# The weights of the first modulation: eight buffers instead of four, and their loads issued in another order

## The chip, the cores and the metric

The kernel runs on one core of a Trainium2 chip. The metric is the time of one execution in microseconds (us). Its engines are PE (TensorE: matmuls; PEld is its weight load), DVE (VectorE), ACT (ScalarE), POOL (GpSimd) and SP (SyncE, which here issues nearly all transfers between HBM and the on-chip memory, in one queue). Each engine takes its instructions in the order in which the program lists them, and waits where one of them is not ready.

## The reference, cut to what matters

One step of a two-layer trunk over T = 1152 tokens (1024 latent tokens, 128 of a prompt) with 1024 features. Of each layer only the beginning matters here:

```
mod = silu(cond) @ w_mod + b_mod                  # six sections of 1024 columns
sh1, sc1, g1, sh2, sc2, g2 = split(mod, 6)
hn  = rms_norm(x, norm1_g) * (1 + sc1) + sh1       # the normalized input
z, xbc, dt, nat_qkv, rwkv_in, diff_qkv = split(hn @ w_in)
... four mixers, an output projection, a squared-ReLU MLP, each gated by a section of mod
```

Nothing can be projected before hn is there; hn needs x, the row norms of x, and the first two sections of mod (sh1 and sc1, 2048 columns) for two conditions, that of the latent tokens and that of the prompt.

## The kernel before, in words

Features lie on the 128 partitions, tokens along the free axis: x is eight tiles of 128 features by 1152 tokens, loaded in three chunks of 384 tokens, two transfers of 768 KB a chunk. Products are made from two halves of each number (`wh`, `wl` of a weight; `h0h`, `h0l` to `h2h`, `h2l` of the normalized chunks 0 to 2), three matmuls for each product (`mm3`, lines 99 to 101).

`modulation_first` (line 169) makes the first two sections of the first layer's modulation on PE. The weights are eight pieces of 128 x 2048 (1 MB each), piece k for features 128k to 128k+127; each takes four matmuls of 512 columns (line 182), which add into four rows in PSUM over all eight pieces. Only after the last piece are the rows copied out (`mrow`), turned into columns by sixteen small transposes (line 192), and added to the bias (`md`, line 194). The pieces lie in a pool with four buffers, so pieces 4 to 7 wait until PE has read pieces 0 to 3. Then come `c_pack` (identity, ones and masks, 549 KB), and, in the program's text after the function, the six loads of x (line 1439).

`norm` does each chunk in two parts. The sums: eight squares on ACT (line 220), added up in turn on DVE and POOL (line 223), six small matmuls (line 227), the inverse root on DVE (lines 229 and 42 to 47, twelve instructions), three transposes on PE (line 233). The application: for each of eight tiles DVE multiplies (`t`, line 240), ACT adds the shift and rounds (lines 242 to 247), and DVE or POOL makes the low half (lines 245 and 248). `proj_fm` then multiplies by weight tiles; the weights come through one `raw` buffer, are split by ACT (`wh`, line 82) and POOL (`wl`, line 84), and the results leave through ACT (`st`, line 262). The first call takes three weight tiles together (72 matmuls a chunk), the second one (24 a chunk); then `proj_tm` takes a weight of two pieces (`in_w_in_tm`). After the norm, `cond_rows` loads the conditions once more (`row`, line 145), and `modulation` makes the other four sections of the first layer on DVE from 32 loads (`mod`, line 159; line 162), while PE projects. A table of relative biases is written to HBM by some twenty small transfers (lines 1152 to 1159).

The order of instructions on each engine is not that of the text: a scheduler places every instruction of the program by its own model of times and by priorities (`high_priority`). What one place changes can so move instructions elsewhere.

Of the memory: the pool `wp` (the weights being split) lies at the right end, and beside it, from `layer_input`, the pool `hn` with the six tiles of the normalized input (six of 12,288 bytes a partition), `stg`, and `nt` with the temporaries of the norm. x and the pool `m0` of `modulation_first` lie on the left.

Of the kernel before, what the change touches and what calls it, by code (L numbers as in the profile page):

```python
# [8 lines left out]
F32 = mybir.dt.float32  # L9
# [5 lines left out]
PSUM = bass.MemoryType.PSUM  # L15
# [5 lines left out]
CH3 = [(0, 384), (384, 384), (768, 384)]  # L21
# [13 lines left out]
def bcast_in(ap, n):  # L35
    return ap.unsqueeze(len(ap.shape)).to_broadcast(list(ap.shape) + [n])
# [75 lines left out]
def ps2(env):  # L112
    return env.ps_d.tile([128, 512], F32, tag="d", name="psd")
# [10 lines left out]
def psx(env):  # L124
    return env.ps_x.tile([128, 512], F32, tag="x", name="psx")
# [40 lines left out]
        nc.vector.tensor_tensor(out=md[:, s], in0=acc[:, :, :, 0], in1=bcast_in(env.bmod[:, L, s * 8:s * 8 + 8], 2), op=ALU.add)  # L166


def modulation_first(env, src, cond, md, pool, psr, pack):

    nc = env.nc
    c = pool.tile([128, 3, 8, 2], F32, name="ccol")
    nc.sync.dma_start(out=c[:, 0], in_=cond)
    nc.scalar.activation(out=c[:, 1], in_=c[:, 0], func=AF.Tanh, scale=0.5)
    nc.vector.scalar_tensor_tensor(out=c[:, 1], in0=c[:, 1], scalar=1.0, in1=c[:, 0], op0=ALU.add, op1=ALU.mult)
    nc.vector.tensor_scalar_mul(out=c[:, 2], in0=c[:, 1], scalar1=0.5)
    rows = [ps2(env), ps2(env)] + [psr.tile([128, 512], F32, name=f"psr{i}") for i in range(2)]
    for k in range(8):
        w = pool.tile([128, 2048], F32, tag="w", name="w", bufs=4)
        nc.sync.dma_start(out=w, in_=src[k])  # L180
        for o in range(4):
            nc.tensor.matmul(rows[o][0:2], c[:, 2, k], w[:, o * 512:o * 512 + 512], start=k == 0, stop=k == 7)
    nc.sync.dma_start(out=pack, in_=env.A["c_pack"])
    r = pool.tile([2, 2048], F32, name="mrow")
    ps = psx(env)
    for o in range(4):
        if o % 2:
            nc.vector.tensor_copy(r[:, o * 512:o * 512 + 512], rows[o][0:2])
        else:
            nc.scalar.activation(out=r[:, o * 512:o * 512 + 512], in_=rows[o][0:2], func=AF.Copy)  # L190
        for j in range(o * 4, o * 4 + 4):
            nc.tensor.transpose(ps[:, 2 * j:2 * j + 2], r[:, j * 128:j * 128 + 128], env.const.ident[0:2, 0:2])
    for s in range(2):
        nc.vector.tensor_tensor(out=md[:, s], in0=ps[:, s * 16:s * 16 + 16].rearrange("p (j c) -> p j c", c=2), in1=bcast_in(env.bmod[:, 0, s * 8:s * 8 + 8], 2), op=ALU.add)
# [12 lines left out]
def hidden(pool, chunks):  # L207

    return [[pool.tile([128, 8, 384], F32R, name=f"h{c}{i}") for i in "hl"] for c in chunks]
# [1176 lines left out]
def kernel(ctx: ExitStack, tc: tile.TileContext, A: dict, O: dict):  # L1386
    nc = tc.nc
    env = Env()
# [18 lines left out]
    cp = const.tile([128, 1098], F32, name="pack")  # L1407
# [10 lines left out]
    def layer_input():  # L1418

        hx, early, tx = ExitStack(), ExitStack(), ExitStack()  # L1420
        hp = hx.enter_context(tc.tile_pool(name="hn", reuse_waits="tile", bufs=1, side="right"))
        env.stg = early.enter_context(tc.tile_pool(name="stg", reuse_waits="tile", bufs=3, side="right"))
        tp = tx.enter_context(tc.tile_pool(name="nt", reuse_waits="tile", bufs=2, side="right"))
        return hidden(hp, range(3)), tp, hx, early, tx

    dense = ExitStack()
    env.wp = dense.enter_context(tc.tile_pool(name="wp", reuse_waits="tile", bufs=1, side="right"))
    H, tp, hx, early, tx = layer_input()
    left = ExitStack()
    xp = left.enter_context(tc.tile_pool(name="xp", reuse_waits="tile", bufs=1))  # L1430
    x = xp.tile([128, 8, T], F32, name="x")
    mds = [const.tile([128, 6, 8, 2], F32, name=f"md{L}") for L in range(DEPTH)]
    start = ExitStack()
    ep = start.enter_context(tc.tile_pool(name="m0", reuse_waits="tile", bufs=1))
    with tc.tile_pool(name="ps_0", reuse_waits="tile", bufs=1, space=PSUM) as ps_0:
        modulation_first(env, A["w_mod0"], A["cond_c"], mds[0], ep, ps_0, cp)
    for c0, n in CH3:
        for k in range(0, 8, 4):
            nc.sync.dma_start(out=x[:, k:k + 4, c0:c0 + n], in_=A["x"][:, k:k + 4, c0:c0 + n])

    for L in range(DEPTH):
        md = mds[L]
# [87 lines left out]
        early = ex.enter_context(tc.tile_pool(name="df_qk", reuse_waits="tile", bufs=1, side="right"))  # L1530
# [4 lines left out]
        with tc.tile_pool(name="ps_t1", reuse_waits="tile", bufs=2, space=PSUM) as ps_t, tc.tile_pool(name="ps_s3", reuse_waits="tile", bufs=1, space=PSUM) as ps_s:  # L1535
            dense, left, hx, tx, mx = ExitStack(), ExitStack(), ExitStack(), ExitStack(), ExitStack()
# [15 lines left out]
        with tc.tile_pool(name="mix", reuse_waits="tile", bufs=1) as mp:  # L1552
# [3 lines left out]
            H = hidden(hx.enter_context(tc.tile_pool(name="hn2", reuse_waits="tile", bufs=1, side="right")), range(1))  # L1556
            tp = tx.enter_context(tc.tile_pool(name="nt2", reuse_waits="tile", bufs=2, side="right"))
# [9 lines left out]
        tp = tx.enter_context(tc.tile_pool(name="nt", reuse_waits="tile", bufs=2, side="right"))  # L1567
# [23 lines left out]
        if nxt:  # L1591
            H, tp, hx, early, tx = nxt
# [142 lines left out]
```

## Time and profile before

| | |
|---|---|
| median of 3 runs | 4220.53 us (4210.94 to 4223.38) |
| the profiled execution | 4216.06 us, of which its span 4214.3 us |
| PE busy | 4039.3 us, 96% of the span |
| DVE busy | 2496.9 us, 59% |
| ACT busy | 1525.2 us, 36% |
| POOL busy | 1110.3 us, 26% |

The profile shows one execution. A busy share is an average over stages with different limits, so what a change of the first hundred microseconds is worth is read from the rows of that stage: from the timeline (each instruction's start and duration, and in brackets the idle time of its engine before it and what ended it), and from windows (busy time of each engine in a stretch, TensorE's granted clock as a share of 2.4 GHz, and what the DMA engines moved).

### The profile page before, as it was taken

The page shows a single profiled execution, that of the slowest core. Times are in us where ns is not written, and L with a number is a line of the kernel's source. Part 1 is how long each engine was busy: PE and PEld are TensorE (multiplying, and loading weights), DVE is VectorE, ACT ScalarE, POOL GpSimd, SP SyncE. Part 2 cuts the span into 40 slices and gives each one's busy share as a digit, 9 for nine tenths or more (in the row PEclk, how much of TensorE's full clock was granted, in tenths as well). Part 3 has the DMA queues.
Part 4 walks back from the last instruction along what each step waited for, and adds up shares of the span by engine and source line. Part 5 has one row for each costly group of instructions (what it writes and reads, how often), then busy time and mean ns, then how long its engine had stood idle before and what let it go on. Part 6 is the DMA issues. An engine that isn't in the chain of part 4 may idle for free.

```text
span 4214.3 us, 69091 instructions
## 1 busy us (share of the span) xinstructions
PE 4039.3 (96%) x27394; PEld 3736.9 (89%) x27394; DVE 2496.9 (59%) x5734; ACT 1525.2 (36%) x2896; POOL 1110.3 (26%) x866
## 2 busy tenths in 40 slices
PE   8899889999999999999999999899899999999999
PEld 5889777877889999999998998778777999999999
DVE  4996747678766993333346647566777463333333
ACT  4333325556644221211243233355566241111111
POOL 2243340223143211211233433302323332112111
PEclk9999989999999999999999999989899999999999
DMA  5663343322231551111144342443122301111112
GB/s 195 197 198 115 119 124 86 91 65 53 70 114 37 170 169 42 41 46 40 46 123 135 114 138 89 136 103 81 38 60 76 106 26 41 46 41 41 45 41 71
DMA packets 211187, 375.74 MB, mean 89 GB/s; under 512 B 78176, under 2 KB 144240, under 8 KB 209840
## 3 DMA queue, kind: packets, MB, share of 16 engines
q1 hardware_dynamic: 210800, 371.31, 29.1%
q8 instruction: 216, 3.54, 0.3%
q14 instruction: 107, 0.88, 0.1%
q0 software_dynamic: 64, 0.02, 0.0%
HBM read 285.33 MB, written 86.42 MB: 88 GB/s over the span
## 4 chain that ended last, share of the span: by engine, by line
PE 76%; DVE 12%; DMA 6%; issue 2%; ACT 2%; SPq 1%; POOL 1%; DVEq 0%; ACTq 0%; POOLq 0%
PE psd L99 12%; PE psd L101 12%; PE psd L100 12%; PE tps L1141 6%; PE psx L101 5%; PE psx L99 5%; PE psx L100 5%; PE tps L1129 2%; DVE junk L162 2%; PE psd L938 2%; PE S L1349 2%; DVE tm L867 1%; DMA K<-scr 1%; PE psd L930 1%; PE psd L958 1%
## 5 line engine op out<-in xcount | busy, mean ns | idle before, releaser
L84 POOL TENSOR_TENSOR wl<-raw,wh 128x1024 fp32r<-128x1024 f32 (+3 forms) x200 | 473.3, 2368 | 1533.6 <-ACT wh L82 1533.6
L82 ACT ACTIVATE wh<-raw 128x1024 fp32r<-128x1024 f32 (+3 forms) x200 | 205.7, 1031 | 770.5 <-PE psd L101 669.5
L294 DVE SCALAR_TENSOR_TENSOR x<-psd,md,x 128x384 f32<-128x384 f32 (+2 forms) x442 | 212.6, 504 | 341.2 <-PE psd L101 340.6
L101 PE MATMUL psd<-fl,wh 128*128 128x384 f32 x992 | 335.2, 338 | 0.0
L99 PE MATMUL psd<-fh,wl 128*128 128x384 f32 x992 | 334.7, 337 | 0.0
L100 PE MATMUL psd<-fh,wh 128*128 128x384 f32 x992 | 334.7, 337 | 0.0
L1141 PE MATMUL tps<-pT,V 128*128 128x128 f32 (+1 forms) x2144 | 299.2, 289 | 1.7 <-ACT pT L1136 1.6
L99 PE MATMUL psd<-h2h,wl 128*128 128x384 f32 x816 | 284.4, 349 | 11.9 <-ACT st L262 7.7
L1141 PEld LDWEIGHTS tps<-pT,V 128*128 128x128 f32 (+1 forms) x2144 | 270.5, 198 | 20.5 <-issue 3.3
L100 PE MATMUL psd<-h2h,wh 128*128 128x384 f32 x816 | 283.3, 348 | 0.0
L101 PE MATMUL psd<-h2l,wh 128*128 128x384 f32 x816 | 281.5, 346 | 0.0
L379 DVE TENSOR_TENSOR fl<-s,fh 128x384 fp32r<-128x384 f32 x192 | 209.2, 1090 | 97.8 <-ACT fh L378 97.4
L1136 ACT ACTIVATE pT<-tps 128x512 f32<-128x512 f32 (+3 forms) x368 | 166.7, 476 | 177.6 <-PE tps L1129 163.3
L99 PE MATMUL psd<-h0h,wl 128*128 128x384 f32 x592 | 206.8, 349 | 1.6 <-ACT st L262 1.3
L377 DVE SCALAR_TENSOR_TENSOR s<-psd,r 128x384 f32<-128x384 f32 x128 | 71.1, 556 | 229.1 <-ACT r L376 228.8
L99 PE MATMUL psd<-h1h,wl 128*128 128x384 f32 x592 | 204.8, 346 | 1.7 <-ACT h1h L244 1.4
L100 PE MATMUL psd<-h0h,wh 128*128 128x384 f32 x592 | 204.2, 345 | 0.0
L100 PE MATMUL psd<-h1h,wh 128*128 128x384 f32 x592 | 203.7, 344 | 0.0
L101 PE MATMUL psd<-h0l,wh 128*128 128x384 f32 x592 | 203.2, 345 | 0.0
L1355 ACT ACTIVATE e<-e,st 128x1280 f32<-128x1280 f32 x144 | 180.5, 1254 | 62.5 <-DVE st L1354 48.7
L101 PE MATMUL psd<-h1l,wh 128*128 128x384 f32 x592 | 202.3, 343 | 0.1
L294 DVE SCALAR_TENSOR_TENSOR x<-psx,md,x 128x384 f32<-128x384 f32 (+2 forms) x198 | 103.4, 538 | 161.6 <-PE psx L101 160.1
(613 smaller groups left out, 10989.3 us busy)
## 6 DMA issues: line engine op xcount, KB each, us to landing
raw<-in_w_ff_dram SPq DMA_DIRECT2D x128, 512.0 KB
mod<-in_w_mod_dram SPq DMA_DIRECT2D x80, 512.0 KB
raw<-in_w_in_fm_dram SPq DMA_DIRECT2D x42, 512.0 KB
scr<-st SPq DMA_DIRECT2D x78, 192.0 KB
scr<-x SPq DMA_DIRECT2D x26, 576.0 KB
K<-scr SPq DMA_DIRECT2D x32, 352.0 KB
K<-scr SPq DMA_DIRECT2D x64, 176.0 KB
u<-scr SPq DMA_DIRECT2D x18, 576.0 KB
```

What stands on the lines that cost most here:

```text
L82: nc.scalar.activation(out=h[:, :n], in_=raw, func=AF.Copy)
L84: nc.gpsimd.tensor_tensor(out=l[:, :n], in0=raw, in1=h[:, :n].bitcast(F32), op=ALU.subtract)
L99: nc.tensor.matmul(ps, al, bh, start=i == 0, stop=False)
L100: nc.tensor.matmul(ps, ah, bh, start=False, stop=False)
L101: nc.tensor.matmul(ps, ah, bl, start=False, stop=i == n - 1)
L162: nc.vector.scalar_tensor_tensor(out=junk, in0=w[:, i * 512:i * 512 + 512], scalar=0.5, in1=parts[c * 2 + i], op0=ALU.mult, op1=ALU.mult, ...
L294: env.nc.vector.scalar_tensor_tensor(out=x[:, kt, s0:s1], in0=ps[:, s0 - c0:s1 - c0], scalar=g[:, kt, cd:cd + 1], in1=x[:, kt, s0:s1], op0 ...
L379: nc.vector.tensor_tensor(out=fl[j][:, c0:c0 + n], in0=s, in1=fh[j][:, c0:c0 + n].bitcast(F32), op=ALU.subtract)
L938: nc.tensor.matmul(pp[:, i * 128:i * 128 + 128], B[hs, c0 + i].rearrange("p a t -> p (a t)"), A[hs, c0 + i].rearrange("p a t -> p (a t)"), ...
L1136: nc.scalar.activation(out=pT[0:g[i][1], i * 128:j * 128], in_=pp[0:g[i][1], i * 128:j * 128], func=AF.Copy)
L1141: nc.tensor.matmul(out, V[0:n, vb], parts[k // 4][0:n, k % 4 * 128:k % 4 * 128 + 128], start=k == 0, stop=k == len(kt) - 1)
L1355: nc.scalar.activation(out=e[:, :N], in_=e[:, :N], func=AF.Exp, scale=-1.0, bias=m, accum_out=st[:, 6:7] if c else s0)
```

## The change

The pieces of the modulation's weights get a pool of their own, `w0`, with eight buffers (65,536 bytes a partition). It lies on the right, and it is closed before `layer_input` is called, so that the tiles of the normalized input come to lie on the same place. The loads are listed as: pieces 0 to 3, `c_pack`, the first chunk of x, pieces 4 to 7, the second and the third chunk of x. No computation is added or taken away.

```diff
-def modulation_first(env, src, cond, md, pool, psr, pack):
+def modulation_first(env, src, cond, md, pool, wpool, psr, pack, load):
...
     for k in range(8):
-        w = pool.tile([128, 2048], F32, tag="w", name="w", bufs=4)
+        if k == 4:
+            nc.sync.dma_start(out=pack, in_=env.A["c_pack"])
+            load(0)
+        w = wpool.tile([128, 2048], F32, tag="w", name="w", bufs=8)
         nc.sync.dma_start(out=w, in_=src[k])
         for o in range(4):
             nc.tensor.matmul(rows[o][0:2], c[:, 2, k], w[:, o * 512:o * 512 + 512], start=k == 0, stop=k == 7)
-    nc.sync.dma_start(out=pack, in_=env.A["c_pack"])
+    load(1)
+    load(2)
...
-    H, tp, hx, early, tx = layer_input()
     left = ExitStack()
...
-    with tc.tile_pool(name="ps_0", reuse_waits="tile", bufs=1, space=PSUM) as ps_0:
-        modulation_first(env, A["w_mod0"], A["cond_c"], mds[0], ep, ps_0, cp)
-    for c0, n in CH3:
+
+    def load(c):
+        c0, n = CH3[c]
         for k in range(0, 8, 4):
             nc.sync.dma_start(out=x[:, k:k + 4, c0:c0 + n], in_=A["x"][:, k:k + 4, c0:c0 + n])
+
+
+    with tc.tile_pool(name="ps_0", reuse_waits="tile", bufs=1, space=PSUM) as ps_0, tc.tile_pool(name="w0", reuse_waits="tile", bufs=1, side="right") as wq:
+        modulation_first(env, A["w_mod0"], A["cond_c"], mds[0], ep, wq, ps_0, cp, load)
+    H, tp, hx, early, tx = layer_input()
```

The first place is SP's queue at the program's start, from the first pieces on (`w` are the pieces, `raw` the weight tiles of the projections). Before:

```order
L180 DMA w<-in_w_mod_dram 128x2048 x4
L183 DMA pack<-in_c_pack_dram 128x1098
L1439 DMA x<-in_x_dram 128x4x384 x4
L91 DMA raw<-in_w_in_fm_dram 128x1024
L1439 DMA x<-in_x_dram 128x4x384 x2
L180 DMA w<-in_w_mod_dram 128x2048 x4
```

and after the change:

```order
L183 DMA w<-in_w_mod_dram 128x2048 x4
L180 DMA pack<-in_c_pack_dram 128x1098
L1442 DMA x<-in_x_dram 128x4x384 x2
L183 DMA w<-in_w_mod_dram 128x2048 x2
L91 DMA raw<-in_w_in_fm_dram 128x1024
L183 DMA w<-in_w_mod_dram 128x2048 x2
L1442 DMA x<-in_x_dram 128x4x384 x4
```

The four last pieces have moved ahead of four of the six loads of x.

The second place is DVE's queue from the modulation's columns (`md`) on: `t` and `h0l` are the application of the norm to chunk 0, `sums` and `st` belong to the sums of a later chunk. Before:

```order
L194 TENSOR_TENSOR md_94<-psx,bmod 128x16 x2
L464 MEMSET sp_1333 128x72
L204 SCALAR_TENSOR_TENSOR md_94<-md_94,ng 128x16
L240 SCALAR_TENSOR_TENSOR t<-x,md_94,psm 128x384 x3
L245 SCALAR_TENSOR_TENSOR h0l<-t,md_94,h0h 128x384
```

and after the change:

```order
L198 TENSOR_TENSOR md_79<-psx,bmod 128x16 x2
L208 SCALAR_TENSOR_TENSOR md_79<-md_79,ng 128x16
L244 SCALAR_TENSOR_TENSOR t<-x,md_79,psm 128x384 x3
L227 TENSOR_TENSOR sums<-sums,sq 128x384
L249 SCALAR_TENSOR_TENSOR h0l<-t,md_79,h0h 128x384 x2
L244 SCALAR_TENSOR_TENSOR t<-x,md_79,psm 128x384 x3
L249 SCALAR_TENSOR_TENSOR h0l<-t,md_79,h0h 128x384
L227 TENSOR_TENSOR sums<-sums,sq 128x384
```

Before, all sums stood ahead of `md` on DVE; now those of chunks 1 (from its second addition on) and 2 stand between the applications.

The third place is SP's queue after the norm: `mod` are the loads of the other sections, `scr` and `in_rel_bias` the small transfers of the bias table, `scr<-st` stores of projected tiles, `in_w_in_tm` the two pieces of the weight of `proj_tm`. Before:

```order
L159 DMA mod<-in_w_mod_dram 128x1024
L1156 DMA scr_236<-in_rel_bias_dram 49x60x16
L159 DMA mod<-in_w_mod_dram 128x1024
L1159 DMA scr_236<-in_rel_bias_dram 60x16 x2
L263 DMA scr_191<-st 128x384
L1159 DMA scr_236<-in_rel_bias_dram 60x16 x4
L159 DMA mod<-in_w_mod_dram 128x1024
L263 DMA scr_192<-st 128x384
L91 DMA raw<-in_w_in_tm_dram 128x1056
```

and after the change:

```order
L159 DMA mod<-in_w_mod_dram 128x1024
L91 DMA raw<-in_w_in_tm_dram 128x1056
L1160 DMA scr_240<-in_rel_bias_dram 49x60x16
L267 DMA scr_197<-st 128x384
L159 DMA mod<-in_w_mod_dram 128x1024
L1163 DMA scr_240<-in_rel_bias_dram 60x16 x6
L159 DMA mod<-in_w_mod_dram 128x1024
L267 DMA scr_198<-st 128x384
L1163 DMA scr_240<-in_rel_bias_dram 60x16 x2
L91 DMA raw<-in_w_in_tm_dram 128x1056
```

The first piece of the weight of `proj_tm` has moved ahead of the bias table's transfers, and the second stands where the table is half written; before, the first stood there.

The scheduler also moved instructions by some tens of places on PE later on: within the first layer up to about a third of PE's instructions, and again in the second layer from a half to four fifths of them. The last fifth of PE's order is the same.

## Rows read from the trace of the kernel before

**Rows 1.** The page: span, and the chain that ended last by engine.
```profile
span 4214.3 us, 69091 instructions
...
PE 76%; DVE 12%; DMA 6%; issue 2%; ACT 2%; SPq 1%; POOL 1%; DVEq 0%; ACTq 0%; POOLq 0%
```
**Rows 2.** Timeline of SP's issues, 5 to 30 us (start, us spent issuing, line, transfer).
```profile
5.67 11.05 SPq L1439 DMA_DIRECT2D x<-in_x_dram  x4
...
18.61 2.42 SPq L1439 DMA_DIRECT2D x<-in_x_dram  x2
21.13 4.94 SPq L180 DMA_DIRECT2D w<-in_w_mod_dram  x4
```
**Rows 3.** Timeline of PE, 9 to 60 us (start, us busy, line, operation, idle before).
```profile
22.11 1.88 PE L182 MATMUL psd<-w,ccol 128*2 128x512 f32 x4
23.83 1.88 PE L182 MATMUL psr<-w,ccol 128*2 128x512 f32 x4
...
36.33 3.57 PE L182 MATMUL psd<-w,ccol 128*2 128x512 f32 x4
...
46.29 1.28 PE L227 MATMUL psm<-pack,sums 128*128 128x1 f32 x10
...
52.65 1.88 PE L182 MATMUL psr<-w,ccol 128*2 128x512 f32 x4
...
58.63 0.65 PE L99 MATMUL psd<-h0h,wl 128*128 128x384 f32 x1
```
**Rows 4.** Windows of 5 us: busy by engine, granted clock, DMA share, GB/s.
```profile
10.00:15.00 5.00, 5.00 (x8) 0.82 (x7) 0.00 (x0) 0.00 (x0) 0.00 (x0) 1.00 1.00 422
...
30.00:35.00 5.00, 1.85 (x9) 1.76 (x9) 2.84 (x11) 2.05 (x5) 2.79 (x2) 0.50 1.04 423
```
**Rows 5.** Timeline of ACT, DVE and POOL around the norm, 20 to 83 us.
```profile
20.25 0.94 ACT L220 ACTIVATE sums<-x 128x384 f32<-128x384 f32 x2 [14.29 <-DMA x<-in_x_dram]
...
24.40 0.56 DVE L223 TENSOR_TENSOR sums<-sums,sq 128x384 f32<-128x384 f32 x1 [2.22 <-ACT sq L220]
...
31.88 0.16 DVE L229 TENSOR_SCALAR st<-psm 128x3 f32<-128x3 f32 x1 [4.08 <-PE psm L227]
...
35.28 0.16 DVE L47 SCALAR_TENSOR_TENSOR st<-st 128x3 f32<-128x3 f32 x1
...
56.61 1.67 DVE L240 SCALAR_TENSOR_TENSOR t<-x,md,psm 128x384 f32<-128x384 f32 x3
...
82.36 1.16 POOL L248 TENSOR_TENSOR h2l<-t,h2h 128x384 fp32r<-128x384 f32 x1 [1.68 <-ACT h2h L247]
82.42 0.22 DVE L245 SCALAR_TENSOR_TENSOR h2l<-t,md,h2h 128x128 fp32r<-128x128 f32 x1
```
**Rows 6.** Timeline of SP's issues, 80 to 122 us.
```profile
83.78 1.66 SPq L145 DMA_DIRECT2D row<-in_cond_dram  x2
...
106.19 0.38 SPq L91 DMA_DIRECT2D raw<-in_w_in_tm_dram  x1
106.62 1.67 SPq L1159 DMA_DIRECT2D scr<-in_rel_bias_dram  x2
...
116.52 0.36 SPq L91 DMA_DIRECT2D raw<-in_w_in_tm_dram  x1
...
118.99 0.65 SPq L432 DMA_DIRECT2D um<-scr  x1
```
**Rows 7.** Timeline of ACT and PE, 108 to 124 us.
```profile
111.14 1.08 ACT L82 ACTIVATE wh<-raw 128x1056 fp32r<-128x1056 f32 x1 [10.20 <-DMA raw<-in_w_in_tm_dram]
...
121.96 0.39 PE L99 MATMUL psd<-wh,h0l 128*128 128x264 f32 x1 [3.28 <-ACT st L262]
```
**Rows 8.** Windows of 50 us: PE, PEld, DVE, ACT, POOL busy, clock, DMA.
```profile
250.00:300.00 50.00, 48.41 (x311) 45.33 (x311) 49.73 (x122) 17.62 (x26) 25.57 (x19) 1.00 0.59 194
...
350.00:400.00 50.00, 46.76 (x350) 42.88 (x349) 29.48 (x90) 12.39 (x28) 18.28 (x22) 0.97 0.22 71
```
**Rows 9.** What PE waited for, 400 to 1300 us: us in total, times, longest.
```profile
PE psm L1066 <- DVE qf L1059: 11.4, 3, 6.3
```

## Prediction, made before the changed kernel was run

> **What bounds the kernel now.** I read the page first. PE is on the chain that ended last for 76% of the span [rows 1], so the change is worth what it takes out of PE's idle time, or what it lets the engines that feed PE do sooner. The change lies in the first 60 us, so the second view is the timeline of that stretch, queue by queue.
>
> SP issues all six loads of x by 21.0 us, and only then, from 21.13 us, the last four pieces of the modulation's weights [rows 2]. PE has finished the first four pieces at 25.7 us (23.83 + 1.88) and takes up the fifth at 36.33, with its clock at 0.50, that is at 1.2 GHz, after the idle stretch from 30 to 35 us; the last piece is done at 54.5 (52.65 + 1.88) and the first projection starts at 58.63 [rows 3, 4]. Meanwhile the DMA engines are full: a share of 1.00 and 422 GB/s at 10 to 15 us, 1.04 and 423 at 30 to 35 [rows 4]. The sums of the norm start when the first half of chunk 0 lands, at 20.25 us, and the application starts at 56.61, when the modulation's columns are there; DVE ends it at 82.6 and POOL at 83.5 [rows 5]. So in the first 58 us the modulation is what is late, since its weights stand behind x. From 56 to 82 us the norm's application on DVE is late, and PE follows it.
>
> The third view is what comes behind the norm. SP can issue the loads of `row` only at 83.78, and the two pieces of the weight of `proj_tm` at 106.19 and 116.52 [rows 6]. ACT stands 10.20 us for the first of these, with the evacuation of PSUM behind it in its queue, and PE takes up work at 121.96 after another wait for that evacuation [rows 7]. Then DVE is the bound for a while: it is busy 49.73 of 50 us at 250 to 300. At 350 to 400 it has slack (29.48) and PE has little (46.76) [rows 8].
>
> **The change part by part.** It adds and removes no instruction; all it costs or gains is order.
>
> The pieces. I start from x's first half, whose place in the queue is the same and which lands at 20.25 us [rows 5]. Behind it now come the second half (0.79 MB), pieces 4 and 5 (1.05 MB each), a weight tile (0.52), and pieces 6 and 7. At 0.42 MB per us [rows 4] piece 4 lands at 20.25 + 1.84/0.42 = 24.6, piece 5 at 27.1, piece 6 at 30.9 and piece 7 at 33.4. PE needs 3.44 us for a piece at full clock (two rows that start 1.72 apart), and ends the fourth at 25.7 [rows 3]; so it needs pieces 4 to 7 at 25.7, 29.1, 34 and 37.4, and waits for none. It does not fall idle, and I take the full clock for it. The end is 25.7 + 4 x 3.44 + 1.4 for the matmuls of the sums that stand between (1.28 for five of the six in the row at 46.29) = 40.9 us, where it was 54.5: 13.6 earlier. What follows is unchanged, so `md` feeds DVE at 43.0 and the first projection starts at 45.0.
>
> The price is chunk 1 and 2 of x, which land at about 37 and 41 us, behind the pieces. The sums of both, which before were done or nearly done when `md` came, now stand among the applications of chunks 0 and 1 on ACT, DVE and POOL. On DVE the application took 82.64 - 56.61 = 26.0 us; added are six additions of 0.56 and one inverse root (from 31.88 to 35.44 at most) [rows 5]: 3.4 + 3.6 = 7.0. Without any new wait the norm would end at 43.0 + 26.0 + 7.0 = 76.0. But each square waits for the addition of the one before, and each of the twelve additions (six on DVE, six on POOL) can stand behind an application's instruction, the longest of which is the one of 1.16 on POOL [rows 5]: 12 x 1.16 = 13.9, hence 89.9. No row shows this mixture. I take a third of it, 4.6, since the chain of chunk 1 begins some six us before `md` and because ACT, which starts each step, has gaps: 80.6, that is 2.0 earlier than before. So of 13.6 us at the first projection 2.0 are left at the norm's end.
>
> The Trainium skill, "DMA: Bandwidth & Descriptors", section on queues, rings and completion order, says that each DMA engine consumes the descriptors of one queue in ring order. The landing of x at 20.25 us, 14.3 us after ACT was free, agrees, as 6.1 MB stood before and in it [rows 5]. It speaks against the change as much as for it, since chunk 1 then pays for every piece put ahead of it (4.7 MB with the weight tile, 11 us at 0.42 MB per us). If the transfers in flight shared the engines evenly instead, chunk 1 would come sooner and piece 7 only near 42 us; by my estimate the first projection would then start near 50, and the sum below would hardly change, as it goes by the norm's end and by SP's queue.
>
> Behind the norm. `row` needs the norm's memory, so it moves with its end: 83.78 - 2.0 = 81.8. Then the scheduler's new order does something of its own: the second piece for `proj_tm` now stands almost where the first one stood (106.19), with two more small transfers ahead of it (1.67) [rows 6]. So it is issued at 106.19 - 2.0 + 1.67 = 105.9 instead of 116.52, 10.6 earlier, and PE restarts at 121.96 - 10.6 = 111.4. For DVE's next work (`um`, loaded at 118.99) SP must first store a tile whose evacuation stands behind that same piece on ACT, at about 112; with two small transfers (1.67) and the 2.5 us that lay between 116.52 and 118.99 that is 116.2, 2.8 earlier.
>
> From there DVE carries its 2.8 us through its full stretch, to about 310 us; PE has a lead of 10.6 which it can use for projections that wait for nothing. Behind that stretch PE is the bound with less left to do. At 390 us the gain is thus between 2.8 and 10.6; I take the middle, 7. The buffers themselves cost nothing: `h0h` is written only after `md`, which needs all pieces read.
>
> The rest of the program does the same work. Where the scheduler has moved instructions I take zero; the nearest row for a bound is PE's wait for `qf`, 11.4 us in three waits [rows 9], which can vanish or double: 11 either way.
>
> The sum: 4216.06 - 7 = 4209 for an execution like the profiled one. That one lies 4.5 below the median of the runs shown, 4220.53, and for the median I forecast 4220.53 - 7 = 4213.5, rounded to 4213. 0.3%, about what a measurement of this kernel can tell from no change, is 12.7 us: 4207.9 to 4233.2.
>
> **The rivals.** (a) More is kept. If the additions fall into gaps, the norm ends at 76.0, 6.6 earlier; then the second piece is issued at 101.3, PE restarts 15.2 earlier, and if DVE's stretch keeps that too the median is 4205. For it: PE is nearly as full as DVE, 48.41 of 50 us at 250 to 300, so a lead should last [rows 8]. Against it: twelve additions on three queues without a wait. (b) The gain is hidden. DVE's full stretch sets the end of the first 310 us, PE's lead turns into waits for DVE behind it, and 2.8 us are left: 4218. For it speaks 49.73 of 50 us on DVE, against it the slack at 350 to 400 [rows 8]. (c) Slower. The additions of chunks 1 and 2 each wait behind two foreign instructions, one of 1.16 on POOL and one on DVE of 0.56 (a third of the 1.67 at 56.61): 12 x 1.72 = 20.6, and the norm ends at 96.6, 14.0 later than before [rows 5]. `row`, the other sections of the modulation and with them DVE's full stretch are later by as much: 4234.5, rounded to 4235. It decides from a norm's end behind 82.6; for it speaks that squares and additions go round three engines, against it that the longest of these instructions would have to stand in the way each time. (d) The pieces are not there in time, because SP's issue of them waits: it spent 11.05 us on four loads of x [rows 2]. PE then has its gap as before, 3 or 4 us shorter, and the result is that of (b).
>
> **How the numbers follow.** The forecast has 0.42, its own range 4205 to 4222 (8 us for the order elsewhere); (a) 0.25, (b) and (d) together 0.20, (c) 0.13. Faster by over 0.3% is most of (a), 0.21, and the lower end of the forecast, 0.12: 0.33. Slower by over 0.3% is most of (c), 0.09, and 0.03 from the order elsewhere: 0.12. The rest, 0.55, is no change. The range of 8 in 10 takes in the order's 11 us below (a)'s middle in part and above (b): 4196 to 4229.
>
> **What would show it.** In the profile after: pieces 4 to 7 issued before chunks 1 and 2; PE without a gap from 9 to 41 us, at full clock; the first projection near 45; chunk 0 applied from 43 on with additions between; the norm's end near 81 (76 for (a), 97 for (c)); the second piece for `proj_tm` issued near 106 and PE's restart near 111; DVE full until about 307. If the norm's end comes at 81 and the time still falls by 13 us or rises, the order of the later parts has done it, and the step "zero elsewhere" is wrong.

## The result, and the profile after

| | before | after |
|---|---|---|
| median of 6 runs each | 4221.52 us (4210.94 to 4225.26) | 4252.84 us (4249.65 to 4264.92) |
| ratio, 95% interval | | 1.0082 [1.0065, 1.0098] |
| the profiled execution | 4216.06 us | 4252.64 us |

The changed kernel is slower, by 4221.5 x 0.0082 = 34.6 us [27.4, 41.4]; I had forecast 4213 and a range of 4196 to 4229. In the lines named here, the line numbers of the new kernel are 3 to 4 higher than before (the norm's application, line 240, is line 244).

The page of the profile after answers to [rows 1]: busy time, then the chain that ended last.

```profile
span 4250.9 us, 69070 instructions
...
PE 4059.8 (96%) x27394; PEld 3750.5 (88%) x27394; DVE 2493.8 (59%) x5734; ACT 1521.2 (36%) x2896; POOL 1117.6 (26%) x866
...
PE 80%; DVE 9%; DMA 5%; issue 2%; ACT 1%; POOL 1%; SPq 1%; DVEq 0%; ACTq 0%; POOLq 0%
```

PE does the same 27,394 matmuls, but is busy 4059.8 us with them instead of 4039.3. So of the 36.6 us between the two spans 20.5 are busy time of PE, and the time is not lost in waits alone: a matmul lasts longer where TensorE's granted clock is at the lower level (1.2 GHz; the four matmuls that started at 36.33 before, in a stretch at 0.50, took 3.57 us [rows 3, 4], and such a four takes 1.88 at 1.00).

The start does what the change says. SP's issues (answer to [rows 2]) have pieces 4 to 7 from 6.87 us on, and chunks 1 and 2 of x behind them:

```profile
5.68 1.15 SPq L1442 DMA_DIRECT2D x<-in_x_dram  x2
6.87 8.50 SPq L183 DMA_DIRECT2D w<-in_w_mod_dram  x2
...
15.90 1.18 SPq L183 DMA_DIRECT2D w<-in_w_mod_dram  x2
18.14 14.07 SPq L1442 DMA_DIRECT2D x<-in_x_dram  x4
```

PE, in the timeline from 9 to 60 us (answer to [rows 3]), goes from piece 4 at 25.19 to the end of piece 7 at 38.91 + 1.88 = 40.8 without a gap, and starts the first projection at 44.19, where it was 58.63:

```profile
25.19 1.88 PE L185 MATMUL psd<-w,ccol 128*2 128x512 f32 x4
...
38.91 1.88 PE L185 MATMUL psr<-w,ccol 128*2 128x512 f32 x4
...
44.19 0.66 PE L99 MATMUL psd<-h0h,wl 128*128 128x384 f32 x1 [1.86 <-ACT h0h L248]
```

But the norm ends later. In the timeline of ACT, DVE and POOL (answer to [rows 5]) the squares of chunk 1 start at 35.79, those of chunk 2 only at 57.51, after ACT has waited until PE had read the sums of chunk 1 (`sums` has one buffer); the application of chunk 1 starts at 64.59, and the last instruction of chunk 2 ends at 88.09 + 1.16 = 89.3, where it was 83.5:

```profile
35.79 0.94 ACT L224 ACTIVATE sums<-x 128x384 f32<-128x384 f32 x2 [6.15 <-DMA x<-in_x_dram]
...
57.51 0.94 ACT L224 ACTIVATE sums<-x 128x384 f32<-128x384 f32 x2 [2.91 <-PE psm L231]
...
42.87 1.66 DVE L244 SCALAR_TENSOR_TENSOR t<-x,md,psm 128x384 f32<-128x384 f32 x3
...
64.59 1.66 DVE L244 SCALAR_TENSOR_TENSOR t<-x,md,psm 128x384 f32<-128x384 f32 x3 [2.69 <-PE psm L237]
...
88.09 1.16 POOL L252 TENSOR_TENSOR h2l<-t,h2h 128x384 fp32r<-128x384 f32 x1 [1.18 <-ACT h2h L251]
```

SP's queue follows the norm's end (answer to [rows 6]): `row` at 89.51 instead of 83.78, `um` at 124.55 instead of 118.99. The second piece for `proj_tm` is issued 2.1 us earlier than before:

```profile
89.51 1.65 SPq L145 DMA_DIRECT2D row<-in_cond_dram  x2
...
98.24 0.41 SPq L91 DMA_DIRECT2D raw<-in_w_in_tm_dram  x1
...
114.42 0.49 SPq L91 DMA_DIRECT2D raw<-in_w_in_tm_dram  x1
...
124.55 0.43 SPq L436 DMA_DIRECT2D um<-scr  x1
```

PE, which had done its projections early, waits 9.68 us behind that piece and restarts at 120.36 (answer to [rows 7]: 121.96):

```profile
119.22 1.08 ACT L82 ACTIVATE wh<-raw 128x1056 fp32r<-128x1056 f32 x1 [13.97 <-DMA raw<-in_w_in_tm_dram]
...
120.36 0.59 PE L99 MATMUL psd<-wh,h0l 128*128 128x264 f32 x1 [9.68 <-ACT wh L82]
```

The windows (answer to [rows 4, 8]) show PE's clock held up in the start, 1.00 instead of 0.50, and DVE's full stretch ending later: at 350 to 400 us it is still busy 37.22 us, where it was 29.48.

```profile
30.00:35.00 5.00, 5.00 (x20) 1.79 (x18) 0.96 (x6) 0.00 (x0) 2.07 (x1) 1.00 1.02 380
250.00:300.00 50.00, 48.15 (x306) 44.33 (x306) 48.47 (x126) 13.77 (x25) 21.17 (x18) 1.00 0.48 147
350.00:400.00 50.00, 49.47 (x357) 45.87 (x356) 37.22 (x100) 14.26 (x25) 22.05 (x24) 0.93 0.37 128
```

To see where the rest is lost I compared when each engine starts the same instruction in both traces. This is the shift of PE's matmuls (median, us, later is positive), by their time in the kernel before; e1 to e3 are experiments below:

```
time before      60-80   380-420  860-900  1350-1400  2400-2450  2800-2850  3450-3500   end
after            -11.0    +12.8    +10.9     +27.2      +27.1      +13.2      +36.6    +36.6
e1                -8.1    +11.3    +10.9     +22.5      +22.3      +25.5      +22.0    +22.0
e2                -0.7     +1.6     -3.3     +18.6      +16.7       +5.5      +23.0    +23.0
e3               -11.0     +6.6     +8.4     +13.1      +13.1      +11.5      +10.0    +10.0
```

PE is 11 us ahead at 60 us and 12.8 behind at 400. Then come three steps far from the change, in stretches whose text is the same: +16 between 870 and 1370, -14 between 2430 and 2820, +23 between 2820 and 3470. Clock and waits differ between two executions of one kernel, so such a step of one trace is a lead and not a measurement; the experiments put times on them.

### The profile page after: what moved, and what is told of

Read it like the earlier page. It is cut to its first block, busy times and chain, and to the rows that moved or that the text cites. A ratio compares the mean times of both kernels' runs of the same rounds, so it can differ in the third digit from the quotient of the medians.

```text
span 4250.9 us, 69070 instructions
## 1 busy us (share of the span) xinstructions
PE 4059.8 (96%) x27394; PEld 3750.5 (88%) x27394; DVE 2493.8 (59%) x5734; ACT 1521.2 (36%) x2896; POOL 1117.6 (26%) x866
## 4 chain that ended last, share of the span: by engine, by line
PE 80%; DVE 9%; DMA 5%; issue 2%; ACT 1%; POOL 1%; SPq 1%; DVEq 0%; ACTq 0%; POOLq 0%
PE psd L99 13%; PE psd L101 12%; PE psd L100 12%; PE tps L1145 6%; PE psx L101 5%; PE psx L99 5%; PE psx L100 5%; PE tps L1133 3%; PE S L1353 2%; PE psd L942 1%; DVE junk L162 1%; PE psd L962 1%; DVE tm L871 1%; PE psd L934 1%; DMA mod<-in_w_mod_dram 1%
```

## The experiments

The theory after the comparison: the time is lost twice, by the norm's later end in the first 130 us, and by the order that the scheduler chose for the rest of the program when the start had moved. The rival was that the lag grows by itself.

**Freezing the order.** To part the two, I wrote down the order of the instructions on every engine as the scheduler had made it for one kernel, and forced it on a part of another. In the text both kernels have the same instructions in the same sequence behind the start, so a table of places is enough:

```diff
     with _tile.TileContext(nc, schedule_with_timeline_sim=True) as tc:
         tile_hybrid_trunk_kernel(tc, A, O)
+        pin(tc)
...
+def pin(tc):          # ORDER: engine -> places, in the order of writing
...
+        for a, b in zip(order, order[1:]):
+            dep(ins[b], ins[a])      # order of issue only, no wait
```

Kernels e1 to e3 and e5 to e12 differ in the table, and in the start where that is said. The traces show that the forcing does what it says: in e6 and e12 PE, DVE and ACT start the same instructions in the same sequence as before, one by one, outside the stretch that was exchanged, and in e2 they do so up to 373 us. That the forcing costs nothing by itself was not timed alone; in e8, the kernel before up to 2840 us, PE is 2.2 us behind at 2400 to 2450 us, inside the scatter of single traces. Ratios are to the kernel before, run on the same chip in the same series (medians 4216.6 to 4219.9); behind each stands what it makes of 4219 us.

**e1, the changed kernel with the old order from 400 us on.**

> The changed kernel, but from about 400 us on every engine issues its instructions in the order that it had in the kernel before (a table of places; the order is forced by edges that wait for nothing). The first 400 us are those of the changed kernel, 12.8 us behind at 400 us. Theory A (the time is lost twice: 13 us by the start itself, and about 24 us by the order that the scheduler chose for the rest): the lag stays near 13 us to the end, 4221 + 13 = 4234 us. Rival B (the start's lag grows by itself, since all that follows works against the same buffers and queues): 4250 us or more, as the changed kernel.

**e2, the mirror of it.**

> The mirror of it: the kernel before, with its own first 400 us, and from there on the order of the changed kernel on every engine. Theory A: nothing up to 400 us, then +15 between 900 and 1300, -12 between 2450 and 2800, +23 between 2850 and 3400 us, so 4221 + 24 = 4245 us. Rival B: no change, 4221 us, within 5 us.

**e3, the changed start alone.**

> The changed kernel's start alone: its first 130 us, and from there on the order of the kernel before. Theory A1 (the lag at 400 us comes from the norm's end, 5 to 6 us later, which the row loads and DVE's full stretch carry on): 4221 + 6 = 4227 us, with a lag near 6 at 400 us. Rival A2 (it comes from the scheduler's order between 130 and 400 us): about 0 at 400 us, 4221. Rival A3 (it comes from PE's wait of 9.7 us for the second weight piece of the token projection): 10 to 13 at 400 us, 4233.

| | median of runs | ratio | us |
|---|---|---|---|
| e1 | 4227.91 | 1.0021 [1.0007, 1.0036] | +9 [3, 15] |
| e2 | 4239.14 | 1.0045 [1.0028, 1.0063] | +19 [12, 27] |
| e3 | 4227.26 | 1.0011 [0.9997, 1.0024] | +5 [-1, 10] |

The theory holds: the later order alone, behind an untouched start, costs 19 us, and without it the changed kernel loses 9. Both together give 28, at the lower end of what was measured for the change (27 to 41). In the table of shifts e1 ends 22 us behind, which looks like the rival's growing lag; but its profiled execution took 4238.33, 10 us above its median, and its growth falls into 870 to 1370 us, where every trace with the old order falls behind that of before (below). e3 says what the start is worth: 5 us by the times, which is not clear of zero, and 6.6 by the shift at 400 us, which is about the lag of the norm's end (5.6) and of `um` (6.1). PE waits there about as long for the second piece of `proj_tm` (9.24 us), and the 10 to 13 us of the third expectation don't come. That e3 has 6.6 and the changed kernel 12.8 at 400 us would be the order between 130 and 400 us (by the times 4 us, which the intervals don't resolve). Six traces whose first 400 us have the order of before scatter from -3.0 to +3.0 there, so a difference of 6 us between two traces is suggested and not shown.

**e4, a small change of another kind.** In the kernel before:

```diff
-        w = pool.tile([128, 2048], F32, tag="w", name="w", bufs=4)
+        w = pool.tile([128, 2048], F32, tag="w", name="w", bufs=3)
```

> The kernel before with three buffers for the first modulation's pieces where it had four. The start changes by little (the fourth piece is issued behind x too, and PE's wait moves, the last piece being the same), but the scheduler chooses another order for a quarter of PE's instructions up to 3200 us. Theory A (the scheduler's choice alone moves the time): a shift of 5 to 25 us of either sign that arises far from the start, in steps of some 10 us at places like 900 to 1300 or 2450 to 3400 us. Rival C (the order's choice is worth less than 5 us in all, and the 24 us are special to the changed kernel's): within 5 us of 4221.

Measured: 4232.45, ratio 1.0027 [1.0017, 1.0037], +11 [7, 16]. At 400 us it is 4.6 behind, at 860 to 900 level again, and in 1350 to 1400 it is 15.5 behind. So a small change of another kind also costs some 10 us, and rival C falls. How much of it is the order alone was not parted here: the step between 870 and 1370 us is one trace's, and old orders show 4 to 12 us there (below).

**e6, e7, e8: one stretch at a time.** The kernel before, with the changed kernel's order in one stretch only.

> The kernel before, with the changed kernel's order on every engine between 2450 and 2840 us alone (second layer). Theory A (a stretch's order has a price of its own that doesn't depend on what stands ahead): the 11 to 14 us that this stretch gave back in the changed kernel are won here, 4220 - 12 = 4208 us. Rival D (that stretch only gave back what earlier stretches had lost, as waits that were there anyway): no change, 4220 us.

> The kernel before, with the changed kernel's order on every engine between 850 and 1350 us alone (first layer). Theory A: 15 to 22 us lost in this stretch and kept, 4220 + 18 = 4238 us. Rival D: the loss is made up for behind, or comes only with what stands ahead: 4220 to 4225 us.

> The kernel before, with the changed kernel's order on every engine between 2840 and 3420 us alone (second layer). Theory A: 15 to 23 us lost in this stretch and kept, 4220 + 18 = 4238 us. Rival D: the stretch lost only what the one ahead of it had won: 4220 to 4226 us.

| | median of runs | ratio | us |
|---|---|---|---|
| e6, 2450 to 2840 us | 4205.80 | 0.9965 [0.9952, 0.9978] | -15 [-20, -9] |
| e7, 850 to 1350 us | 4230.80 | 1.0027 [1.0017, 1.0038] | +11 [7, 16] |
| e8, 2840 to 3420 us | 4244.90 | 1.0057 [1.0044, 1.0070] | +24 [19, 30] |

Rival D falls in all three: each stretch has its own price. Theory A's sizes fit in e6 and e8; e7's 11 is less than the 18 that it had. Within the intervals the prices add up (-15 + 11 + 24 = 20, e2 has 19). e6 is faster than both kernels.

The traces say the same. This is how far PE's shift against the trace of before changes over each stretch (us, from table windows like those above), by whether a kernel has the new or the old order in it:

| stretch | new order | old order |
|---|---|---|
| 870 to 1370 us | +16 to +22 (after, e2, e7) | +4 to +12 (e1, e3, e5, e6, e8 to e12) |
| 2430 to 2820 us | -14 to -7 (after, e2, e6, e10, e11) | -3 to +6 (e1, e3, e5, e7, e8, e9, e12) |
| 2820 to 3470 us | +18 to +24 (after, e2, e8) | -5 to -1 (e1, e3, e5, e6, e7, e9, e10, e11) |

New and old orders don't overlap in any of the three. In the first stretch the old orders fall behind too, so the trace of before took less time there than the others do, and part of the step of +16 was that.

What a price consists of can be seen in e8. These are PE's waits from 2840 to 3440 us before (us in total, times, longest):

```profile
PE psx L979 <- ACT st L984: 4.5, 3, 2.7
PE S L1349 <- DMA K<-scr: 3.8, 1, 3.8
PE S L1349 <- issue: 2.7, 1, 2.7
```

and these in e8:

```profile
PE tps L1129 <- POOL e L1367: 7.0, 4, 3.1
PE S L1349 <- DMA Q<-scr: 5.2, 1, 5.2
PE S L1349 <- DVE e L1352: 4.1, 5, 1.4
PE S L1232 <- DMA K<-scr: 3.7, 1, 3.7
PE psd L768 <- DMA sg<-scr: 3.5, 1, 3.5
```

A pair of loads of Q and K now stands some rows later in SP's queue, and PE waits 5.2 us for Q (1.4 before); POOL's share of the attention weights (line 1367) is asked for before it is done, four times, for 7.0 us in total (once, for 1.0, before). Each is small; what they and the longer matmuls come to together is read from the windows, columns as in [rows 8]: before

```profile
2450.00:2840.00 390.00, 365.08 (x2813) 316.46 (x2811) 234.70 (x551) 161.29 (x349) 104.35 (x108) 0.92 0.41 116
2840.00:3420.00 580.00, 546.42 (x4395) 474.36 (x4390) 406.41 (x1042) 313.23 (x591) 173.56 (x147) 0.96 0.25 68
```

the second stretch in e8, moved by its shift:

```profile
2846.00:3448.00 602.00, 556.81 (x4397) 480.65 (x4397) 407.75 (x1044) 314.09 (x592) 176.63 (x148) 0.95 0.24 65
```

Of 602 - 580 = 22 us, 556.81 - 546.42 = 10.4 are matmuls that last longer, and 11.6 idle time of PE. In e6's trace the stretch of 390 us takes 383:

```profile
2458.00:2841.00 383.00, 360.05 (x2793) 313.02 (x2793) 231.38 (x546) 158.43 (x345) 103.61 (x108) 0.93 0.42 117
```

Here 5.0 of the 7 us are busy time of PE and 2.0 idle time (its profiled execution took 4212.16, the median being 4205.80). The mean granted clock of the span goes the same way in e6, 0.969 in the mean of its runs against 0.966 in those of the kernel before; for a PE that is busy nearly always that would be worth some 0.003 x 4214 = 12.6 us (an estimate from these three numbers, each clock being rounded to 0.001). But this estimate is no account of the prices in general: in e2 the means are 0.9657 and 0.9661, which is 2 us of its 19, and e4, 11 us slower, has the higher clock (0.9666 against 0.9661).

How far one trace can be trusted is shown by e6's first stretch too, 850 to 1350 us, where its order is that of before. Before:

```profile
850.00:1350.00 500.00, 472.18 (x3829) 411.11 (x3828) 355.12 (x899) 272.10 (x502) 150.73 (x124) 0.97 0.25 71
```

e6:

```profile
849.00:1360.00 511.00, 483.15 (x3831) 420.22 (x3829) 354.40 (x898) 272.35 (x502) 150.97 (x124) 0.95 0.25 70
```

The same instructions in the same order took 11 us more, at a granted clock of 0.95 instead of 0.97. A single pair of traces had shown me +16 for the new order in this stretch; the times say +11 [7, 16].

**e12, the last stretch cut in two.**

> Where in 2840 to 3420 us the 24 us are lost: the kernel before with the changed kernel's order between 3100 and 3420 us alone. In the profile of the whole stretch 4.7 us were lost up to 3100 and 16.3 behind. Theory A (each part has its own price): 4219 + 16 = 4235 us. Rival F (the loss needs the first part, where a pair of Q and K loads is issued later and PE waits for it): 4219 to 4224 us.

Measured: 4232.44, ratio 1.0034 [1.0019, 1.0050], +14 [8, 21]. So the part behind 3100 us has a price of its own, as theory A says, and rival F falls. The rest, some 10 us, would belong to the part ahead of it, which wasn't run alone; it is a difference of two times, each uncertain by 5 to 7 us. Which engine's order carries the price wasn't tried: with orders mixed within a stretch, one engine can wait for what another holds back.

**e5, chunk 1 of x ahead of pieces 4 to 7,** old order from 130 us.

```diff
             load(0)
+            load(1)
...
-    load(1)
     load(2)
```

> The changed kernel with chunk 1 of x loaded ahead of the last four pieces (chunk 2 stays behind them), and with the order of the kernel before from 130 us on. It differs from the start tried alone only in the start. Theory A1 (the norm's end is late because the sums of chunk 1 begin only when that chunk lands, at 35.8 us, and each chunk's chain of squares, inverse root and application runs one behind the other): chunk 1's sums are done near 43 us, the first projection still starts near 45, the norm ends at 73 to 77 instead of 89, the loads of the rows are issued at 74 to 79 (before: 83.8), and the time is 4220 - 7 = 4213 us. Rival A4 (what counts is that chunks' sums and applications share three engines, whenever the chunk lands): the norm ends at 84 to 89, and the time is 4220 to 4226.

Measured: 4220.66, ratio 1.0003 [0.9992, 1.0014], +1 [-3, 6]. The norm ended at 87.1, the number of A4, but by another way than either theory said: the scheduler put the sums' matmuls of chunk 0 ahead of piece 4 on PE (31.54 instead of 25.19), and `md` came at 52.9 instead of 42.4. So this does not tell A1 from A4; it says that in this version chunk 1 came early (its squares at 31.2 instead of 35.8) and the modulation late.

**e9, the sums of chunks 1 and 2 taken out,** old order from 130 us.

```diff
-        for k in range(8):
+        for k in range(2 if short and c else 8):    # short: the first norm of the first layer
             sq = tp.tile(...)
```

> The changed kernel's start with the order of the kernel before from 130 us on, as in the start tried alone, but six of the eight squares and all additions of chunks 1 and 2 are left out of the first layer's first norm (so its sums are short; this is a measurement of their cost alone). Theory A1 (the additions of chunks 1 and 2 between the applications set the norm's end, and the norm's end sets the lag at 400 us): application from 43 us without additions, norm's end at 70 to 75 instead of 88 to 89, rows' loads issued near 75, the lag at 400 us goes from +6 to about -8, and 4219 - 8 = 4211 us. Rival A5 (the lag at 400 us is set by something that the norm's end doesn't move, as the order of the loads on SP's queue or PE's wait for the token projection's second piece): the norm ends as early, but the lag at 400 us stays above 0, and the time at 4220 to 4227 us.

Measured: 4214.90, ratio 0.9991 [0.9977, 1.0005], -4 [-10, 2], which does not tell the two theories apart. The norm's end, POOL's last `h2l`, went from 89.2 in e3 (first line) to 79.5 in e9:

```profile
87.99 1.16 POOL L252 TENSOR_TENSOR h2l<-t,h2h 128x384 fp32r<-128x384 f32 x1 [1.17 <-ACT h2h L251]
...
78.49 1.01 POOL L252 TENSOR_TENSOR h2l<-t,h2h 128x384 fp32r<-128x384 f32 x1 [1.66 <-ACT h2h L251]
```

The lag at 400 us went from +6.6 to -4.6. So the lag moves with the norm's end, and rival A5 falls. But 79.5 is not the 70 to 75 that I expected. The application takes longer than before even without any addition in it. Before, from its first instruction to the norm's end:

```profile
56.60:83.50 26.90, 24.94 (x136) 24.66 (x137) 25.04 (x61) 22.99 (x49) 13.53 (x13) 0.94 0.08 30
```

and in e9:

```profile
43.85:79.50 35.65, 32.74 (x157) 31.78 (x158) 30.48 (x68) 23.51 (x50) 14.95 (x13) 0.81 0.13 44
```

35.65 us instead of 26.90. DVE is busy in 30.48 of them instead of 25.04, and these 5.4 us are all in the inverse roots, whose steps stand in this stretch: 18 steps take 8.3 us here, where before 12 took 2.8. Six are more, and the rest is steps that last longer beside POOL (last section). The other 3.3 us are idle time of DVE, 2.8 of them one wait ahead of chunk 2's application, at 68.58.

**e10 and e11, versions meant to be faster than both kernels.** e10 has chunk 1 between pieces 5 and 6, and e6's order behind 130 us; e11 is e6 with the new order between 400 and 700 us too (the table alone).

```diff
             load(0)
+        if k == 6:
+            load(1)
...
-    load(1)
     load(2)
```

> A version meant to be faster than both kernels: eight buffers, chunk 1 of x loaded between the second and the third of the last four pieces, behind 130 us the order of the kernel before, except for 2450 to 2840 us, where the changed kernel's order stands. The later part alone gave 4206 us. Theory A1: chunk 1's sums are done before or near the modulation's end (48 to 50 us), the norm ends at 77 to 81 instead of 83, the lag at 400 us is -2 to -5, and the time 4202 to 4204 us. Rival A4 (the norm's end doesn't follow the modulation's end at all, since three chains of sums of some 13 us each and the applications share the same engines): norm's end at 84 to 88, lag +2 to +5, time 4207 to 4211 us.

> A second version meant to be faster than both kernels: the kernel before, with the changed kernel's order between 400 and 700 us and between 2450 and 2840 us. In the profile of the kernel with the new order from 400 us on, PE was 7 us ahead at 700 us. Theory A (prices of stretches add up): 4206 - 7 = 4199 us. Rival E (the 7 us at 700 us were a shorter time at the lower clock in that one execution, 37.5 us in 400 to 650 where the kernel before had 58.0, and not the order): 4206 us, as with the second stretch alone.

Measured: e10 4209.57, ratio 0.9983 [0.9969, 0.9996]; e11 4206.53, ratio 0.9972 [0.9959, 0.9985]. In e10 the norm ends at 86.1, in A4's range, though the lag at 400 us is -2.1, as A1 had it; the time gains nothing on e6. e11 gains nothing either, as rival E has it; its order differs from that of before only from 604 us on, so there was little that could have gained. The best version found is e6, 15 us [9, 20] faster than before, and nothing of it comes from the early pieces.

## Why the prediction was wrong

Step by step, in its own order:

- The pieces, right. PE without a gap to 40.8 (forecast 40.9), DVE's application from 42.87 (43.0), the first projection at 44.19 (45.0), chunk 1 at 35.79 (about 37).
- The norm's end, wrong: 88.4 on DVE (89.2 on POOL) instead of 80.6. I had added 26.0 for the application [rows 5], 3.4 for the additions and 3.6 for a second inverse root on DVE, and 4.6 for waits. e9 parts them anew. Without additions DVE takes 78.39 - 43.85 = 34.5 us for the application and the inverse roots in it, where 26.0 + 3.6 had been taken: 4.9 too little. The additions of chunks 1 and 2 with their waits then cost about 10 (the norm's end in e3 less that in e9, 89.2 - 79.5 = 9.7; e9 starts 1.0 later), where 3.4 + 4.6 had been taken: 2 to 3 too little. So both terms were too small, the larger error being the 26.0 carried over from a stretch in which the sums of two chunks were done or nearly done, and no weight was being split on POOL beside it. The third that was taken for the waits had no row behind it, as the prediction says of itself. Rival (c) had the right sign and the right place, and "decides from a norm's end behind 82.6" held, but its price of 14 us was too high: 5 to 6.
- Behind the norm, right but for that. From `row` to the second piece it is 114.42 - 89.51 = 24.9 (forecast 24.1), from there to PE's restart 5.9 (5.5), and from there `um` comes 10.1 behind the piece (10.3).
- The gain at 390 us, "between 2.8 and 10.6, the middle": not borne out, since there was a loss, and how PE's lead counts stays open. In e3 `um` is 6.1 us late and PE's restart 1.6 early, and it is 6.6 behind at 400 us; in e9 `um` is 3.6 early and the restart 8.1 early, and it is 4.6 ahead. Both speak for DVE's stretch, as rival (b) had it. But in e5 (`um` 4.5 late, restart 0.9 early, 2.2 behind) and e10 (`um` 2.4 late, restart 3.0 early, 2.1 ahead) the lag lies between the two, and single traces scatter by 3 us there.
- "Where the scheduler has moved instructions I take zero", 11 either way: this is the step that made the forecast wrong by most. The order beyond 400 us alone cost 19 us [12, 27] (e2); that of 130 to 400 us may have cost another 4 to 6, which the times don't resolve. With the old order behind the start (e3, 4227.26) the time would have been inside the stated range, though not at its 4213. The wait for `qf`, from which I had taken the bound [rows 9], hardly moved:

```profile
PE psm L1070 <- DVE qf L1063: 10.0, 3, 4.8
```

  The bound was the wrong kind of number. It took one wait, where a new order changes many small ones and the busy time of PE in stretches of 400 to 600 us: -15, +11 and +24 us in three stretches.

I had named the order of the later parts as what would make "zero elsewhere" wrong, though beside a norm's end of 81 that did not come, but gave it only 11 us. What stays open: e1 and e2 together leave some 7 us of the 34.6 unexplained, inside their intervals; which moved instructions carry most of each stretch's price; and how much of it is granted clock.

## What to carry to other kernels

Where a scheduler places the whole program, a change of the first 60 us can buy a new order far behind it (here up to 3420 us), and in this kernel that lottery (-15 to +24 us a stretch) was larger than the edit itself (e3: 5 us [-1, 10]): freeze the order behind the edit, measure the edit alone, and then try orders as changes of their own. A duration taken over from the old trace holds only beside the same neighbours: 26.9 us of application became 35.7 when it started 13 us earlier, with six more steps of inverse roots in it. And a lead of one engine is not to be counted in full where another engine bounds the next stretch: in e3 PE restarted 1.6 us early, DVE's `um` came 6.1 late, and PE was 6.6 behind at 400 us.

## What the runs showed of the hardware that I had not expected

**Beside an instruction of POOL, some DVE instructions last until POOL's has ended, however small they are.** The timeline of DVE and POOL in the changed kernel, 47 to 53 us:

```profile
48.01 2.65 DVE L249 SCALAR_TENSOR_TENSOR h0l<-t,md,h0h 128x384 fp32r<-128x384 f32 x1 [0.37 <-ACT h0h L248]
50.58 1.34 DVE L227 TENSOR_TENSOR sums<-sums,sq 128x384 f32<-128x384 f32 x1
...
47.87 2.38 POOL L84 TENSOR_TENSOR wl<-raw,wh 128x1024 fp32r<-128x1024 f32 x1
50.20 2.59 POOL L252 TENSOR_TENSOR h0l<-t,h0h 128x384 fp32r<-128x384 f32 x2
```

An `h0l` takes 0.61 alone (two from 44.92 take 1.15 together) and 2.65 here, where POOL splits the third weight until 50.25; the addition takes 0.55 alone, at 44.45, and 1.34 here, where the first of POOL's two ends at 50.20 + 1.30 = 51.50. Steps of the inverse roots, which take 0.16 us alone, show it most. In the kernel before:

```profile
33.28 0.99 DVE L47 SCALAR_TENSOR_TENSOR st<-st 128x3 f32<-128x3 f32 x1
...
33.26 0.99 POOL L223 TENSOR_TENSOR sums<-sums,sq 128x384 f32<-128x384 f32 x1 [1.46 <-ACT sq L220]
```

and in e9:

```profile
48.01 2.32 DVE L47 SCALAR_TENSOR_TENSOR st<-st 128x3 f32<-128x3 f32 x1
...
47.63 2.67 POOL L84 TENSOR_TENSOR wl<-raw,wh 128x1024 fp32r<-128x1024 f32 x1
```

It doesn't hold for every DVE instruction: `t`, one of whose inputs PE has written into PSUM (`psm`), takes 0.60 at 51.84 in the changed kernel, inside POOL's instruction from 51.47 to 52.79. The Trainium skill, "SBUF — State Buffer", section "SBUF: two separate sides", says that DVE, for an operation with two inputs in SBUF, and GpSimd take a shared pair of ports as an exclusive lock for a whole instruction; these rows agree. It is part of what made 26.9 us into 35.7.

**The same program scatters by its clock.** 23 runs of the kernel before, in one series on one chip, had spans from 4204.2 us at a mean granted clock of 0.969 to 4229.7 at 0.963, with a correlation of -0.91 between the two (-0.80 to -0.87 in the other three series). A difference of 0.3% between two single executions says nothing here, since these runs lie 0.6% apart; with a dozen runs beside 23 to 29 of the kernel before, the intervals were 0.10 to 0.16% to either side.
